# Half an output projection beside the last attention block, a router on un-normed rows, and GpSimd work in short pieces

## The chip, the cores and the metric

The kernel runs on one core of a Trainium2 chip. The metric is the device time of one execution in microseconds; the median of several executions counts. A core has TensorE (PE, matrix products into PSUM), VectorE (DVE), ScalarE (ACT), GpSimd (POOL) and SyncE (SP, which here only issues loads). Each engine works through its own instructions in order; semaphores make one engine wait for another.

## The reference

A decoder trunk of two layers on 1024 tokens (T) of width 1024 (D), all in float32. Cut to what matters here:

```python
for layer in range(DEPTH):
    if layer % 2 == 0:   # RWKV-7 (8 heads) and chunked GLA (4 heads)
        mix = concat([rwkv(h @ w_in), gla(h @ w_in)]) @ w_out
    else:                # S5 (32 groups) and chunked HGRN2 (4 heads)
        mix = concat([s5(h @ w_in), hgrn2(h @ w_in)]) @ w_out
    h = _layer_norm(DN_ALPHA * h + mix, ln1_g[layer], ln1_b[layer])
    ffn = _hierarchical_moe(h, ...)   # top-1 of 4 groups, top-2 of 8 experts in it
    h = _layer_norm(DN_ALPHA * h + ffn, ln2_g[layer], ln2_b[layer])

# GLA and HGRN2, per chunk: S <- diag(exp(b_last)) S + k_dec^T v;  o = (q exp(b)) S + scores v
# router: coarse = softmax(x @ wg + bg); fine = softmax(x @ we[group] + be[group])
```

## The kernel before, in words

The kernel is written with a tile framework. A planner in it gives every engine its order of instructions when the kernel is built, from the order of the program and a model of what each takes; so a line that is moved in the program may move work on all engines, and the order has to be read from the built program.

Float32 products are made from two parts. `split` (L104) rounds an operand to a "high" part on ScalarE (L106) and subtracts it to get the "low" part, on VectorE or, for weights of the input and output projections, on GpSimd (L107); three matmuls (hi·hi, lo·hi, hi·lo) then give one product. One weight part is 128 x 1024 elements; for the input projections it holds 8 slices of the contraction, for 128 output columns (`proj_T`, L164 to L166), 24 matmuls for 512 tokens.

A layer goes: mixers (tokens in two halves of 512, `n` = 0, 1), output projection with the first norm and the router (`out_ln1`, L685), routing (`route`, L781, whose second half, `overflow`, L878, places rows beyond an expert's capacity), 32 experts (`moe`, L1021), and `combine` with the second norm.

`gla_core` (L501) does a block of two heads (GLA) or one (HGRN2). For the levels s = 0, 1, 2, 4 ... 64 of a chunk of 128, TensorE makes the scores of the level (L522, L524) in PSUM banks of the ring "iv", VectorE copies them under a mask into the score tile (L532; the last level by ScalarE, L529), and VectorE multiplies gK and gQ for the next level by the decays (L541, L542). Then come the state (L551, L555) and the outputs (L560, L561), a norm of the output (L563 to L569), and a store to the scratch tensor `ydram` by GpSimd's queue (L76).

Before the last GLA block of layer 0, `last` frees the input projection's tiles, and `out_weights` (L674) loads the eight parts of the output weights (SP, L681; four raw buffers `oraw`) and splits them (ScalarE woh, GpSimd wol).

`out_ln1` then goes over eight tiles of 128 rows. `project` loads the residual row `or` (L692) and the mixers' outputs `oyr` from `ydram` (L694), splits them (oyh, oyl) and makes the product in two halves of 24 matmuls (L702 to L704); L705 adds the residual. `finish`, one tile behind, normalizes (`layer_norm`: statistics L661, L662, ScalarE L663, L664, L666, then VectorE's L667 and L668), stores the rows to `hdram`, transposes them (L716), and multiplies them with the router weights (L720, L721).

An expert's weights come as quarters of 128 x 1024, split by ScalarE and VectorE (`w_split`, `cut`) into two rings: the first HL quarters during `out_ln1`, the next HL2 when `moe` begins. `ex_in` transposes the gathered rows and makes xh and xl (L924 and after); `ex_up` (L938 to L940) multiplies. `keep` and `self.kept` chain instructions of an engine so that the planner leaves their order as written.

Of the kernel before, what the change touches and what calls it, by code (L numbers as in the profile page):

```python
# [20 lines left out]
D = 1024  # L21
NT = 8
# [13 lines left out]
class Kern:  # L36
# [67 lines left out]
    def split(self, hi, lo, src, lo_engine=None):  # L104
        nc = self.nc
        self.keep(nc.scalar.activation(hi, src, AF.Copy))  # L106
        self.keep((lo_engine or nc.vector).tensor_tensor(lo, src, hi.bitcast(F32), op=OP.subtract))  # L107
# [120 lines left out]
    def rwkv_setup(self):  # L228
# [14 lines left out]
        self.rwkv_consts(cst)  # L243
# [4 lines left out]
        lora = cst.tile([128, 2, 512], F32, name="lora")  # L248
# [9 lines left out]
        for i in range(2):  # L258
            Q, Zd = cst.tile([128, 8, 4, 64], F32, name=f"Q{i}"), cst.tile([128, 8, 2, 64], F32, name=f"Zd{i}")
# [241 lines left out]
    def gla_core(self, n, q, k, f, heads, S, norm_g, store):  # L501
# [8 lines left out]
        for s in (0, 1, 2, 4, 8, 16, 32, 64):  # L510
            L, R = (k if s < 2 else Ke), Q if s else q
            ps = [self.bank("iv", (128, 4, 128)) for _ in heads]
# [12 lines left out]
            for i, p in enumerate(ps):  # L525
                if s == 64:
                    nc.scalar.activation(SC[i][0:64, :, 64:], p[0:64], AF.Copy)
                elif s == 0:
                    nc.vector.tensor_tensor(SC[i], p, self.ident[:, None, :].to_broadcast([128, 4, 128]), op=OP.mult)  # L529
                else:  # L530
                    m = self.glev[s].rearrange("p (b t) -> p b t", t=s)[:, None].to_broadcast([128, 4, 64 // s, s])
                    nc.vector.copy_predicated(SC[i].rearrange("p c (b t) -> p c b t", t=2 * s)[:, :, :, s:], m,  # L532
                                              p.rearrange("p c (b t) -> p c b t", t=s))
            if s:
# [10 lines left out]
                nc.vector.tensor_tensor(d, d2[:, :, 0], d2[:, :, 1], op=OP.mult)  # L545
        kdT = self.token_major(Ke, "gkdT")
# [49 lines left out]
    def gla(self, n, hT, ydram, last):  # L596
# [17 lines left out]
        for blk in range(2):  # L614
# [40 lines left out]
    def layer_norm(self, pool, r, g, b, out, engine=None):  # L655
# [9 lines left out]
        nc.vector.scalar_tensor_tensor(rs[:, 1:2], mv[:, 0:1], -1.0, rs[:, 0:1], op0=OP.mult, op1=OP.mult)  # L665
        nc.scalar.activation(r, r, AF.Identity, scale=rs[:, 0:1], bias=rs[:, 1:2])  # L666
        nc.vector.tensor_tensor(r, r, g, op=OP.mult)  # L667
        (engine or nc.gpsimd).tensor_tensor(out, r, b, op=OP.add)  # L668
# [5 lines left out]
    def out_weights(self, l, w_out):  # L674

        es = ExitStack()
        pool = es.enter_context(self.tc.tile_pool(name=f"ow{l}", bufs=1, side="right", reuse_waits="tile"))
        raws = [pool.tile([128, D], F32, name=f"oraw{i}") for i in range(4)]
        W = [tuple(pool.tile([128, D], F32R, name=f"wo{x}{k}") for x in "hl") for k in range(KT)]
        for k in range(KT):  # L680
            self.nc.sync.dma_start(raws[k % 4], w_out[128 * k:128 * k + 128, :])  # L681
            self.split(W[k][0], W[k][1], raws[k % 4], self.nc.gpsimd)
        return es, W

    def out_ln1(self, l, src, ydram, W, hdram, ypool, pool):  # L685
# [3 lines left out]
        def project(i):  # L689
            ts = slice(128 * i, 128 * i + 128)  # L690
            r = pool.tile([128, D], F32, tag="or", bufs=3, name="or")
            nc.sync.dma_start(r, self.rows(src, i))  # L692
            yr = ypool.tile([128, KT, 128], F32, tag="oyr", bufs=2, name="oyr")
            nc.sync.dma_start(yr, ydram.rearrange("k p t -> p k t")[:, :, ts])  # L694
            yh = ypool.tile([128, KT, 128], F32R, tag="oyh", bufs=2, name="oyh")
            yl = ypool.tile([128, KT, 128], F32R, tag="oyl", bufs=2, name="oyl")
            self.split(yh, yl, yr)
            for q in range(2):
                ds_ = slice(512 * q, 512 * q + 512)
                p = self.bank("pj")  # L700
                for k, (wh, wl) in enumerate(W):
                    nc.tensor.matmul(p, yh[:, k, :], wh[:, ds_], start=(k == 0), stop=False)  # L702
                    nc.tensor.matmul(p, yh[:, k, :], wl[:, ds_], start=False, stop=False)  # L703
                    nc.tensor.matmul(p, yl[:, k, :], wh[:, ds_], start=False, stop=(k == KT - 1))  # L704
                nc.vector.scalar_tensor_tensor(r[:, ds_], r[:, ds_], ALPHA, p, op0=OP.mult, op1=OP.add)  # L705
            return r

        def finish(i, h):
            self.layer_norm(pool, h, g, b, h, nc.vector)
            self.store(self.rows(hdram, i), h)  # L710
# [10 lines left out]
            nc.vector.tensor_tensor(L[:, i, :], p[:, :36], bias, op=OP.add)  # L721

        for i in range(NT + 1):
            h = project(i) if i < NT else None
            if i == 0:
                g = self.bcast_row(pool, a["ln1_g"][l], "ln1g")
# [996 lines left out]
```

## Time and profile before

| what | value |
|---|---|
| median of 3 runs | 2972.58 us (2968.28 to 2976.91) |
| the profiled execution's own time | 2965.17 us |
| its span | 2963.4 us |
| TensorE busy | 2669.8 us (90% of the span) |
| VectorE busy | 2149.8 us (73%) |
| ScalarE busy | 1583.1 us (53%) |
| GpSimd busy | 739.3 us (25%) |
| granted TensorE clock, mean | 0.941 |

The stages of that execution: layer 0's mixers until about 770 us, its last GLA block 770 to 833, output projection and router 832 to 961, routing until 977, experts 987 to 1565, combine and layer 1's mixers until 2187, output stage 2147 to 2290, experts 2320 to 2893, combine until the end. In 40 equal slices of the span (tenths of busy time, 9 is 90% or more) the page shows:

```profile
PE   8999999999689699999997787879988799999995
DVE  5775447764444899999995658887554899999985
PEclk9999999999779799999998898889989899999998
```

A row of the timeline says when an instruction began and what it took; in brackets stands how long its engine had been idle and what ended that. A row with a count stands for several instructions in succession.

### The profile page before, as it was taken

What the parts mean: (1) busy time and instruction counts of PE and PEld (TensorE: products, weight loads), DVE (VectorE), ACT (ScalarE), POOL (GpSimd) and SP (SyncE); (2) the same over time, 40 slices, a digit from 0 to 9 for tenths busy, and PEclk for the clock granted to TensorE, in tenths of its full rate; (3) what the DMA queues carried; (4) which work ended last, traced back from release to release, by engine and by line L of the source; (5) the groups of instructions that cost most, each with busy time, mean ns of one, the idle gap of its engine ahead of it and who ended that gap; (6) DMA issues with size and microseconds to landing.
All of it is one profiled execution on the core that took longest, in us unless ns stands there. A gap on an engine that the chain in (4) does not pass through costs nothing.

```text
span 2963.4 us, 40755 instructions
## 1 busy us (share of the span) xinstructions
PE 2669.8 (90%) x15284; PEld 1977.1 (67%) x15284; DVE 2149.8 (73%) x3204; ACT 1583.1 (53%) x2292; POOL 739.3 (25%) x619
## 2 busy tenths in 40 slices
PE   8999999999689699999997787879988799999995
PEld 6766676666567477777774576667777577777772
DVE  5775447764444899999995658887554899999985
ACT  4342343333322588888883333334533588888873
POOL 4222222323300211111103454452130111111103
PEclk9999999999779799999998898889989899999998
DMA  3111131011253799999987322122343799999985
GB/s 109 30 37 33 43 87 38 27 29 47 78 175 140 256 376 379 375 380 376 382 334 223 96 74 57 44 69 74 127 153 135 275 376 378 382 383 378 381 315 196
DMA packets 234064, 581.52 MB, mean 196 GB/s; under 512 B 47534, under 2 KB 156167, under 8 KB 184711
## 3 DMA queue, kind: packets, MB, share of 16 engines
q1 hardware_dynamic: 211718, 518.03, 49.2%
q0 software_dynamic: 22144, 60.85, 5.8%
q8 instruction: 122, 2.00, 0.3%
q14 instruction: 80, 0.65, 0.1%
HBM read 541.97 MB, written 52.43 MB: 201 GB/s over the span
## 4 chain that ended last, share of the span: by engine, by line
issue 37%; PE 29%; DVE 12%; POOL 7%; ACT 2%; DMA 2%; POOLq 0%; SPq 0%; DVEq 0%; ACTq 0%
POOL xg L912 4%; PE bpj L164 3%; PE bpj L165 3%; PE bpj L166 3%; PE biv L522 2%; PE bpj L704 2%; PE bpj L702 2%; PE bpj L703 2%; POOL ybuf L976 2%; PE biv L414 1%; DVE gQ L542 1%; PE bpp L720 1%; PE bpo L171 1%; DVE gK L541 1%; DMA xg<-hdram,gi 1%
## 5 line engine op out<-in xcount | busy, mean ns | idle before, releaser
L107 DVE TENSOR_TENSOR mlo<-raw,mhi 128x1024 fp32r<-128x1024 f32 x768 | 923.9, 1222 | 109.2 <-ACT mhi L106 75.0
L106 ACT ACTIVATE mhi<-raw 128x1024 fp32r<-128x1024 f32 x768 | 805.9, 1059 | 201.6 <-PE bpo L969 87.2
L164 PE MATMUL bpj<-hT_hi,whi 128*128 128x512 f32 x736 | 310.7, 422 | 10.7 <-DVE hq L577 9.0
L107 POOL TENSOR_TENSOR wlo<-wraw,whi 128x1024 fp32r<-128x1024 f32 x92 | 221.5, 2409 | 392.7 <-ACT whi L106 324.5
L166 PE MATMUL bpj<-hT_hi,wlo 128*128 128x512 f32 x736 | 307.0, 417 | 9.4 <-POOL wlo L107 9.4
L165 PE MATMUL bpj<-hT_lo,whi 128*128 128x512 f32 x736 | 307.9, 418 | 0.0
L912 POOL DMA_INDIRECT xg<-hdram,gi x64 | 136.3, 2130 | 646.4 <-PE by L924 602.9
L106 ACT ACTIVATE whi<-wraw 128x1024 fp32r<-128x1024 f32 x92 | 97.1, 1057 | 233.2 <-PE bpj L165 161.7
L940 PE MATMUL bpj<-mhi,xl 128*96 128x512 f32 x512 | 203.5, 397 | 0.8 <-DVE xl L107 0.8
L938 PE MATMUL bpj<-mhi,xh 128*96 128x512 f32 x512 | 203.2, 397 | 0.0
L939 PE MATMUL bpj<-mlo,xh 128*96 128x512 f32 x512 | 202.7, 396 | 0.0
L938 PE MATMUL biv<-mhi,xh 128*96 128x512 f32 x512 | 201.8, 394 | 0.0
L939 PE MATMUL biv<-mlo,xh 128*96 128x512 f32 x512 | 201.6, 394 | 0.0
L940 PE MATMUL biv<-mhi,xl 128*96 128x512 f32 x512 | 201.6, 394 | 0.0
L164 PEld LDWEIGHTS bpj<-hT_hi,whi 128*128 128x128 f32 x736 | 143.9, 196 | 46.5 <-DVE hq L577 10.3
L166 PEld LDWEIGHTS bpj<-hT_hi,wlo 128*128 128x128 f32 x736 | 143.6, 195 | 40.9 <-POOL wlo L107 11.4
L165 PEld LDWEIGHTS bpj<-hT_lo,whi 128*128 128x128 f32 x736 | 143.5, 195 | 29.3 <-issue 3.5
L976 POOL DMA_INDIRECT ybuf<-yo,si x64 | 60.2, 940 | 385.2 <-ACT yo L975 375.5
L522 PE MATMUL biv<-gQ,gK 64*128 64x64 f32 (+1 forms) x640 | 76.1, 311 | 58.6 <-DVE gQ L542 58.6
L522 PEld LDWEIGHTS biv<-gQ,gK 64*128 64x128 f32 (+1 forms) x640 | 69.7, 222 | 74.3 <-issue 41.9
L704 PE MATMUL bpj<-woh,oyl 128*128 128x512 f32 x256 | 103.1, 403 | 7.8 <-DVE oyl L107 7.8
L940 PEld LDWEIGHTS bpj<-mhi,xl 128*96 128x96 f32 x512 | 83.4, 163 | 37.6 <-DVE xl L107 1.8
(608 smaller groups left out, 5717.0 us busy)
## 6 DMA issues: line engine op xcount, KB each, us to landing
raw<-in_moe_w_dram SPq DMA_DIRECT2D x384, 1024.0 KB
wraw<-in_ab_w_in_dram SPq DMA_DIRECT2D x50, 512.0 KB
wraw<-in_cd_w_in_dram SPq DMA_DIRECT2D x40, 512.0 KB
cy<-ybuf SPq DMA_DIRECT2D x16, 1024.0 KB
oyr<-ydram SPq DMA_DIRECT2D x16, 512.0 KB
hdram<-or POOLq DMA_DIRECT2D x16, 512.0 KB, 2.9
lnh<-hdram SPq DMA_DIRECT2D x16, 512.0 KB
ydram<-go POOLq DMA_DIRECT2D x16, 256.0 KB, 2.8
```

Of the source, the lines that this page charges most:

```text
L106: self.keep(nc.scalar.activation(hi, src, AF.Copy))
L107: self.keep((lo_engine or nc.vector).tensor_tensor(lo, src, hi.bitcast(F32), op=OP.subtract))
L164: nc.tensor.matmul(dst, wh[:, k, :], xh[:, k, :], start=(k == 0), stop=False)
L165: nc.tensor.matmul(dst, wh[:, k, :], xl[:, k, :], start=False, stop=False)
L166: nc.tensor.matmul(dst, wl[:, k, :], xh[:, k, :], start=False, stop=(k == KT - 1))
L522: nc.tensor.matmul(p[:, c, :], L[r, cc], rhs, start=True, stop=True)
L704: nc.tensor.matmul(p, yl[:, k, :], wh[:, ds_], start=False, stop=(k == KT - 1))
L912: self.nc.gpsimd.indirect_dma_start(out=xg[:CAP, :], out_offset=None, in_=hdram, in_offset=bass.IndirectOffsetOnAxis(ap=gidx, axis=0), bou ...
L938: self.keep(self.nc.tensor.matmul(p, xh[:, k, :], wh, start=(k == 0), stop=False))
L939: self.keep(self.nc.tensor.matmul(p, xh[:, k, :], wl, start=False, stop=False))
L940: self.keep(self.nc.tensor.matmul(p, xl[:, k, :], wh, start=False, stop=(k == KT - 1)))
L976: return nc.gpsimd.indirect_dma_start(out=ybuf, out_offset=bass.IndirectOffsetOnAxis(ap=sidx, axis=0), in_=y, in_offset=None, bounds_check ...
```

## The change

- **Short pieces.** GpSimd's low part of 128 x 1024 becomes four instructions of 128 x 256 (`lo_part`), and so does GpSimd's add of the second norm.
- **GLA levels.** The score banks get a ring "gs" with a turn of its own (the same two banks; four in the last GLA block of layer 0). The multiplies for the next level stand ahead of the masked copies of this one.
- **Output weights and early tiles.** The parts are loaded after the last block's core in program order (`out_early`), through two raw buffers. In layer 0 row tiles 0 to 3 (tokens 0 to 511) are projected there too. The other tiles run two ahead of `finish`, with four `or` buffers and one `oyr`.
- **Router.** `finish` transposes the un-normed row. The router weights are multiplied by ln1_g; sums of the weights and the part of ln1_b come from 16 matmuls with ones. The logits are p·rs + (sums·(-mu·rs) + bias), two VectorE operations. The norm is applied, and the row stored, after that.
- **First parts of the experts.** `cut` makes the high part and returns the low part as a function to be called. At the start of `moe` the low parts of the second ring come after `overflow`'s last multiply and after xl.
- RWKV constants, Q, Zd and lora move into a pool that is freed before the last block.

The diff, cut to its core:

```diff
+    def lo_part(self, hi, lo, src, lo_engine=None):
+        if lo_engine is None:
+            self.keep(self.nc.vector.tensor_tensor(lo, src, hi.bitcast(F32), op=OP.subtract))
+            return
+        hi, lo, src = (x if len(x.shape) == 2 else x.rearrange("p a b -> p (a b)") for x in (hi, lo, src))
+        n = hi.shape[1]
+        for i in range(0, n, n // 4):
+            s = slice(i, i + n // 4)
+            lo_engine.tensor_tensor(lo[:, s], src[:, s], hi[:, s].bitcast(F32), op=OP.subtract)
...
-            ps = [self.bank("iv", (128, 4, 128)) for _ in heads]
+            ps = [self.bank("gs", (128, 4, 128)) for _ in heads]
...
-    RINGS = dict(pj="ab", iv="cd", pp="e", po="f", y="g", ch="h")
+    RINGS = dict(pj="ab", iv="cd", gs="cd", pp="e", po="f", y="g", ch="h")
...
+        for i in range(0, D, D // 4):
+            s = slice(i, i + D // 4)
+            nc.gpsimd.tensor_tensor(out[:, s], r[:, s], b[:, s], op=OP.add)
...
-        raws = [pool.tile([128, D], F32, name=f"oraw{i}") for i in range(4)]
+        def part(k):
+            raw = p.tile([128, D], F32, tag="oraw", bufs=2, name="oraw")
+            self.nc.sync.dma_start(raw, w_out[128 * k:128 * k + 128, :])
+            self.split(W[k][0], W[k][1], raw, self.nc.gpsimd)
+        return es, W, part, pool
...
+    def out_early(self, l, src, ydram, weights, tiles):
+        es, W, part, pool = weights
         for k in range(KT):
+            part(k)
+        self.opool = pool("oe")
+        self.projected = {i: self.project(i, src, ydram, W, self.opool) for i in tiles}
...
         def finish(i, h):
-            self.layer_norm(pool, h, g, b, h, nc.vector)
-            self.store(self.rows(hdram, i), h)
+            rs = self.norm_stats(pool, h)
...
-            nc.vector.tensor_tensor(L[:, i, :], p[:, :36], bias, op=OP.add)
+            t = pool.tile([128, 36], F32, tag="lgt", bufs=2, name="lgt")
+            nc.vector.scalar_tensor_tensor(t, sums, rs[:, 1:2], bias, op0=OP.mult, op1=OP.add)
+            nc.vector.scalar_tensor_tensor(L[:, i, :], p[:, :36], rs[:, 0:1], t, op0=OP.mult, op1=OP.add)
+            self.norm_apply(h, rs, g, b, h, nc.vector)
+            self.store(self.rows(hdram, i), h)
+        done = self.projected
+        at = len(done)
+        for i in range(NT):
+            while at < min(NT, i + 2):
+                done[at] = self.project(at, src, ydram, W, self.opool)
+                at += 1
+            finish(i, done.pop(i))
...
-        for j in range(HL, HL + HL2):
-            cut(j)
+        low = [cut(j) for j in range(HL, HL + HL2)]
...
+        self.kept = {self.last_over.ins.engine: self.last_over}
         more()
-        self.kept = {}
+        for f in low:
+            f()
...
             def last():
                 es.close()
                 close()
+                self.rings["gs"] = "cdeh"
...
+            ahead()
...
+                        lambda: self.out_early(0, x, yd[0], weights[0], range(4)))
...
+        self.out_early(1, mid, yd[1], weights[1], ())
```

TensorE in the last GLA block of layer 0. bgs and biv are the score banks, by the state and output banks, woh and wol the output weights' parts, oyh and oyl those of a row tile. Before, the block's matmuls stand by themselves:

```order
L522 MATMUL biv<-gQ,gK 128x64 x40
L524 MATMUL biv<-gQ,gK 64x64 x8
L496 MATMUL biv<-ident,gK 128x128 x4
L551 MATMUL by<-gV,gkdT 64x128 x8
L560 MATMUL by<-gQ,glS 128x128
```

Now:

```order
L533 MATMUL bgs<-gQ,gK 128x64 x24
L728 MATMUL bpj<-woh_7071,oyh 128x512
L729 MATMUL bpj<-wol_7072,oyh 128x512
L728 MATMUL bpj<-woh_7071,oyh 128x512
L729 MATMUL bpj<-wol_7072,oyh 128x512
L533 MATMUL bgs<-gQ,gK 128x64 x8
L730 MATMUL bpj<-woh_7071,oyl 128x512
L728 MATMUL bpj<-woh_7073,oyh 128x512
L729 MATMUL bpj<-wol_7074,oyh 128x512
L533 MATMUL bgs<-gQ,gK 128x64 x8
```

The first weight parts of tile 0 now stand between the levels, ahead of the levels 16, 32 and 64; farther on the block's state stands behind the fifth part, its outputs behind the sixth and seventh, and the matmul of its last norm behind the eighth. Tiles 1 to 3 follow it.

VectorE at the end of `out_ln1`, from the last tile's aggregate to the first operation of routing. Before:

```order
L662 BN_AGGR lnmv<-lnst 128x2
L721 TENSOR_TENSOR logits<-bpp,gbias 128x36
L665 SCALAR_TENSOR_TENSOR lnrs<-lnmv,lnrs 128x1
L667 TENSOR_TENSOR or<-or,ln1g 128x1024
L668 TENSOR_TENSOR or<-or,ln1b 128x1024
L721 TENSOR_TENSOR logits<-bpp,gbias 128x36
L794 TENSOR_REDUCE mx<-logits 128x8
```

Now:

```order
L678 SCALAR_TENSOR_TENSOR lnrs<-lnmv,lnrs 128x1
L686 TENSOR_TENSOR or<-or,ln1b 128x1024
L787 SCALAR_TENSOR_TENSOR lgt<-gsums,lnrs,gbias 128x36
L684 TENSOR_TENSOR or<-or,ln1g 128x1024
L788 SCALAR_TENSOR_TENSOR logits<-bpp,lnrs,lgt 128x36
L686 TENSOR_TENSOR or<-or,ln1b 128x1024
L852 TENSOR_REDUCE mx<-logits 128x8
```

The last logits stand between the two passes of the norm, no longer behind both and the transposes.

VectorE at the start of the experts (om and rm are `overflow`'s last steps, mlo the low part of an expert's weights, xl that of the gathered rows). Before:

```order
L107 TENSOR_TENSOR mlo<-raw_8136,mhi 128x1024
L895 CAST exi<-ex 128x22
L901 SCALAR_TENSOR_TENSOR blk<-blk,rq 128x16
L107 TENSOR_TENSOR mlo<-raw_8136,mhi 128x1024
L904 TENSOR_TENSOR om<-e_1080,blk 128x336
L107 TENSOR_TENSOR mlo<-raw_8138,mhi 128x1024
L905 TENSOR_TENSOR rm<-om,v_8029 128x336
L107 TENSOR_TENSOR xl<-bch,xh 128x384
```

Now:

```order
L959 SCALAR_TENSOR_TENSOR blk<-blk,rq 128x16
L953 CAST exi<-ex 128x22
L962 TENSOR_TENSOR om<-e_1095,blk 128x336
L963 TENSOR_TENSOR rm<-om,v_8255 128x336
L111 TENSOR_TENSOR xl<-bch,xh 128x384
L111 TENSOR_TENSOR xl<-by,xh 128x384
L919 SCALAR_TENSOR_TENSOR emiv<-biv,slotp 96x21
L111 TENSOR_TENSOR mlo<-raw,mhi 128x1024
```

All eight low parts of the second ring stand behind xl.

## Rows read from the trace of the kernel before

**Rows 1.** Windows: busy us of PE, PEld, DVE, ACT, POOL; granted clock; DMA share; GB/s.

```profile
770.00:833.00 63.00, 36.50 (x201) 26.94 (x199) 25.27 (x37) 17.19 (x23) 23.02 (x14) 0.56 0.33 103
...
841.00:948.00 107.00, 106.63 (x526) 88.86 (x527) 52.32 (x77) 27.17 (x42) 3.74 (x7) 0.98 0.41 137
...
1000.00:1550.00 550.00, 548.83 (x2570) 396.62 (x2569) 499.39 (x490) 457.61 (x550) 86.74 (x58) 1.00 0.99 373
...
1720.00:2000.00 280.00, 224.03 (x1272) 184.36 (x1271) 225.00 (x416) 95.30 (x169) 139.15 (x99) 0.90 0.21 58
```

**Rows 2.** Timeline, end of the last GLA block of layer 0: start, duration, engine, line, operation.

```profile
832.94 0.54 POOL L76 DMA_DIRECT2D ydram<-go  x1 [6.18 <-DVE go L611]
...
841.19 0.80 PE L704 MATMUL bpj<-woh,oyl 128*128 128x512 f32 x1 [7.83 <-DVE oyl L107]
```

**Rows 3.** Timeline, the same block's first part: the output weights and two VectorE multiplies.

```profile
777.08 16.94 POOL L107 TENSOR_TENSOR wol<-oraw,woh 128x1024 fp32r<-128x1024 f32 x7 [11.70 <-ACT woh L106]
...
779.47 7.62 SPq L681 DMA_DIRECT2D oraw<-in_ab_w_out_dram  x4
...
783.18 1.06 ACT L106 ACTIVATE woh<-oraw 128x1024 fp32r<-128x1024 f32 x1 [3.35 <-DMA oraw<-in_ab_w_out_dram]
...
784.45 2.57 DVE L542 TENSOR_TENSOR gQ<-gQ,gD 128x256 f32<-128x256 f32 x1
...
797.43 0.42 DVE L542 TENSOR_TENSOR gQ<-gQ,gD 128x256 f32<-128x256 f32 x1
```

**Rows 4.** Timeline, two neighbouring matmuls of the projection at full clock.

```profile
947.75 0.39 PE L703 MATMUL bpj<-wol,oyh 128*128 128x512 f32 x1
...
947.97 0.40 PE L704 MATMUL bpj<-woh,oyl 128*128 128x512 f32 x1
```

**Rows 5.** Timeline, end of the output stage of layer 0: last tile, router, first routing operation.

```profile
948.41 0.69 DVE L705 SCALAR_TENSOR_TENSOR or<-or,bpj 128x512 f32<-128x512 f32 x1 [4.03 <-PE bpj L704]
...
954.35 1.23 DVE L668 TENSOR_TENSOR or<-or,ln1b 128x1024 f32<-128x1024 f32 x1
...
955.62 1.12 PE L716 MATMUL bpp<-ident,or 128*128 128x128 f32 x4 [4.15 <-DVE or L668]
...
961.32 0.19 DVE L794 TENSOR_REDUCE mx<-logits 128x8 f32<-128x32 f32 x1
```

**Rows 6.** Timeline, start of the expert stage of layer 0.

```profile
985.32 0.88 PE L924 MATMUL bch<-ident,xg 96*128 96x96 f32 x4 [9.37 <-DMA xg<-hdram,gi]
...
986.30 0.49 ACT L106 ACTIVATE xh<-bch 128x384 fp32r<-128x384 f32 x1 [17.05 <-PE bch L924]
...
990.16 0.55 DVE L107 TENSOR_TENSOR xl<-bch,xh 128x384 fp32r<-128x384 f32 x1
...
991.53 0.72 PE L940 MATMUL bpj<-mhi,xl 128*96 128x512 f32 x1
```

**Rows 7.** Groups of instructions, whole span, shapes kept apart: count, busy us, mean ns, idle before.

```profile
L107 POOL TENSOR_TENSOR wlo<-wraw,whi 128x1024 fp32r<-128x1024 f32 x92 | 221.5, 2409 | 392.7 <-ACT whi L106 324.5 <-PE bpj L166 29.8 <-PE biv L522 19.6
...
L540 POOL COPY gK<-hk 128x256 f32<-128x256 f32 x8 | 6.7, 837 | 18.0 <-DVE hk L1249 18.0
...
L541 DVE TENSOR_TENSOR gK<-gK,gD 128x256 f32<-128x256 f32 x72 | 51.2, 711 | 6.0 <-PE biv L524 6.0
```

**Rows 8.** Timeline, HGRN2 beside S5 in layer 1: GpSimd operations back to back, and VectorE.

```profile
1804.47 1.17 POOL L1464 TENSOR_TENSOR stmp<-s5C,s5PI 128x576 f32<-128x576 f32 x1
...
1804.87 1.05 DVE L541 TENSOR_TENSOR gK<-gK,gD 128x256 f32<-128x256 f32 x1
...
1805.72 1.47 POOL L1465 TENSOR_TENSOR sCA<-sCA,stmp 128x576 f32<-128x576 f32 x1
```

**Rows 9.** What TensorE waited for in layer 1's mixers, 1720 to 2145 us.

```profile
PE biv L522 <- DVE gQ L542: 23.6, 16, 8.3
...
PE bpj L166 <- POOL wlo L107: 6.6, 2, 4.5
```

**Rows 10.** The same for layer 0's mixers, 40 to 770 us.

```profile
PE biv L522 <- DVE gQ L542: 10.2, 7, 4.4
```

**Rows 11.** Timeline, last HGRN2 block of layer 1.

```profile
2153.04 1.94 PE L522 MATMUL biv<-gQ,gK 128*128 128x64 f32 x8 [4.80 <-DVE gQ L542]
```

More of the change, by code (lines that the diff above doesn't have):

```diff
@@ new lines, in part, with project @@
+        def part(k):
[3 more added lines that the diff above has]
+        return es, W, part, pool
+    def project(self, i, src, ydram, W, pool):
+        nc = self.nc
+        ts = slice(128 * i, 128 * i + 128)
+        r = pool.tile([128, D], F32, tag="or", bufs=4, name="or")
+        nc.sync.dma_start(r, self.rows(src, i))
+        yr = pool.tile([128, KT, 128], F32, tag="oyr", bufs=1, name="oyr")
+        nc.sync.dma_start(yr, ydram.rearrange("k p t -> p k t")[:, :, ts])
+        yh = pool.tile([128, KT, 128], F32R, tag="oyh", bufs=2, name="oyh")
+        yl = pool.tile([128, KT, 128], F32R, tag="oyl", bufs=2, name="oyl")
+        self.split(yh, yl, yr)
+        for q in range(2):
+            ds_ = slice(512 * q, 512 * q + 512)
+            p = self.bank("pj")
+            for k, (wh, wl) in enumerate(W):
+                nc.tensor.matmul(p, yh[:, k, :], wh[:, ds_], start=(k == 0), stop=False)
+                nc.tensor.matmul(p, yh[:, k, :], wl[:, ds_], start=False, stop=False)
+                nc.tensor.matmul(p, yl[:, k, :], wh[:, ds_], start=False, stop=(k == KT - 1))
+            nc.vector.scalar_tensor_tensor(r[:, ds_], r[:, ds_], ALPHA, p, op0=OP.mult, op1=OP.add)
+        return r
@@ L686, in out_ln1 @@
+    def out_ln1(self, l, src, ydram, W, hdram, pool):
         nc, a = self.nc, self.a
         L = self.rpool.tile([128, NT, 36], F32, name="logits")
[L689 to L706, printed above, removed]
@@ new lines, in out_ln1 @@
+        for x, j in ((wb, 1), (wge, 0)):
+            nc.vector.tensor_tensor(x, wge, gb[:, j, :, None].to_broadcast([128, KT, 36]), op=OP.mult)
+        bias = pool.tile([128, 36], F32, name="gbias")
+        nc.sync.dma_start(bias[:, 0:4], a["moe_bg"][l].rearrange("(o n) -> o n", o=1).to_broadcast([128, 4]))
+        nc.sync.dma_start(bias[:, 4:], a["moe_be"][l].rearrange("g e -> (g e)").rearrange("(o n) -> o n", o=1).to_broadcast([128, 32]))
+        p = self.bank("pp")
+        for j, x in enumerate((wge, wb)):
+            for k in range(KT):
+                nc.tensor.matmul(p[:, 36 * j:36 * j + 36], self.ones, x[:, k, :], start=(k == 0), stop=(k == KT - 1))
@@ L708, in finish @@
+        sums = pool.tile([128, 36], F32, name="gsums")
+        nc.vector.tensor_copy(sums, p[:, 0:36])
+        nc.vector.tensor_tensor(bias, bias, p[:, 36:72], op=OP.add)
         def finish(i, h):
-            self.layer_norm(pool, h, g, b, h, nc.vector)
-            self.store(self.rows(hdram, i), h)
+            rs = self.norm_stats(pool, h)
             hT = pool.tile([128, KT, 128], F32, tag="ohT", bufs=2, name="ohT")
@@ L1018, in cut @@
         if j < 2 * len(self.halves):
-            self.parts[j] = self.w_split(self.raws[j // 2], j % 2, self.halves[j // 2][0].shape[1])
+            self.parts[j], low = self.w_split(self.raws[j // 2], j % 2, self.halves[j // 2][0].shape[1])
+            return low
+        return lambda: None
     def moe(self, l, pool, gi, si, exi, hdram, ybuf):
@@ L1102, in moe_more @@
                 for z in range(4):
-                    self.ex_up(x, ph[w], z, self.w_split(raws[w][z // 2], z % 2, 512))
+                    part, low = self.w_split(raws[w][z // 2], z % 2, 512)
+                    low()
+                    self.ex_up(x, ph[w], z, part)
             raws.append([self.w_load(ws[2], q) for q in range(2)])
@@ L1110, in moe_more @@
             for z in range(4):
-                self.ex_down(h, py, z, self.w_split(raws[2][z // 2], z % 2, 1024))
+                part, low = self.w_split(raws[2][z // 2], z % 2, 1024)
+                low()
+                self.ex_down(h, py, z, part)
             self.ex_out(py, ix[:, 1:2], ybuf)
```

102 lines of the change are left out of this document (51 added, 51 removed).

## The prediction

> **What bounds the kernel now.** I read the 40 slices of the page first: TensorE is busy 90% of the span, so a change can only win where its row drops below 9. Then the stages one by one. In the expert stage TensorE is busy 548.8 of 550 us at full clock with the DMA engines at 0.99 [rows 1]: nothing of the change can shorten that stage itself, only the way into it. The output projection of layer 0 is also a full stretch: 106.6 of 107 us from 841 to 948. What lies idle is the stretch before it, the last GLA block of layer 0 (770 to 833), where TensorE works 36.5 of 63 us at a granted clock of 0.56, and layer 1's mixers, where it works 224 of 280 us and VectorE 225 [rows 1].
>
> The timeline says why the projection starts only at 841: the block's last result is stored at 832.94, and the next real matmul waits for VectorE's oyl, which had waited for the load of that store [rows 2]. Row tiles 0 to 3 need nothing of this block: it computes tokens 512 to 1023. Then the waits in the mixers: the longest sum in layer 1 is for gQ, a VectorE multiply, 23.6 us in 16 waits, the largest 8.3 [rows 9]; in layer 0 the same line stands with 10.2 us [rows 10].
>
> **Projection of four tiles beside the last block (layer 0).** A tile is 8 weight parts x 3 matmuls x 2 halves = 48 matmuls, 0.22 to 0.23 us apart at full clock [rows 4], so 10.8 us; four are 43 us. The question is when these four are done. The added price is that the weights now pass through 2 raw buffers, not 4, and that by the new order TensorE meets them between the block's levels. One buffer's round [rows 3]: high part 1.06 us, low part 16.94/7 = 2.42, and 3.7 us from the re-load's issue (779.47) to the next high part (783.18), together 7.2 us. Two buffers give a part each 3.6 us. The first low part ends at 779.5; the eighth then at 779.5 + 7 x 3.6 = 804.7, where before the queue was through at about 796.5 (a part per 2.42 us). By the order the block's last norm matmul stands behind the eighth part of tile 0, so its store goes out near 812 instead of 832.94, and with the 8 us from store to matmul [rows 2], tiles 4 to 7 can start from about 820. Tile 0 ends near 807. Tiles 1 to 3 follow without a wait, 32.4 us and some 2 us for a clock still low at their start: 842. So at 842 four tiles are left, where before at 841.2 all eight were left: 43 - 1 = **42 us gained**. Does the block itself fit? Its 36.5 us of TensorE work were at 0.56 of the clock, about 20 us at full clock [rows 1]; with 10.8 of tile 0 that is 31 us for the 34 us from 771 to 805 if the clock rises, so this is tight. Bounds: -50 (everything dense at full clock from 771: 20 + 43 us of work end at 834) and -22 (clock and weights hold tile 0 until about 826).
>
> **Router from un-normed rows.** Before, the last tile's transposes wait 4.15 us for the normed row, and routing begins at 961.32 [rows 5]. Now they need only the residual sum, which is ready 0.69 us after 948.41. The transposes, copies and small matmuls then run beside the norm's chain, and what stays ahead of routing on VectorE is that chain, whose last add ends at 954.35 + 1.23 = 955.6 [rows 5]. So routing starts 5.7 us earlier; the two small operations on 36 columns take the place of one. The row's store is not in the way: routing lasts until the gather. Per layer -5.5, **together -11** (-6 to -12; layer 1 by the same code). The 16 added matmuls with ones and the scaled router weights stand among other work; I cost them at nothing. If that cover were gone, they would cost 16 matmuls of 36 columns, under 4 us per layer by the pitch of [rows 4].
>
> **First parts of the experts.** The gathered rows arrive at 985.32, but VectorE makes xl only at 990.16, behind overflow operations and weight low parts mixed with them; the first matmul on xl is at 991.53 [rows 6]. In the new order xl comes ahead of the low parts of the second ring. It could start after the transposes (0.88 us) and one copy (0.49 us), 986.7; add the same 1.37 us from xl to matmul: 988.1. **-3 per layer, -6** (0 to -8). The low parts pushed back are VectorE's; it has 50.6 us to spare in the 550 us behind [rows 1], and if that were not enough, TensorE would wait at the second expert for what was gained here.
>
> **Short pieces.** VectorE's multiply takes 0.42 us alone and 2.57 us while GpSimd works through the weights' low parts [rows 3]; the mean of 72 is 0.71 [rows 7]. A GpSimd low part holds 2.41 us, 92 times, for the input weights alone [rows 7]. Does a waiting VectorE get in between two GpSimd operations that stand back to back? The trace says yes [rows 8]: the multiply at 1804.87 ends 1805.92, just behind the GpSimd operation that ended at 1805.64, though the next one was queued. A piece of 128x256 is bounded by 0.60 us (a quarter of 2.41) and by 0.84 us (a copy of this size, which shares the time with VectorE) [rows 7]; I take 0.65, by the first, since it is the same operation. So the longest single wait falls from 2.1 us to about 0.6. It doesn't vanish: a chain of VectorE operations meets four short waits instead of one. I take half of what TensorE waits for gQ: **-12 in layer 1** of 23.6 [rows 9], **-5 in layer 0** of 10.2 [rows 10]. In layer 1's last block, where two waits in a row are like the one of 4.80 us [rows 11], **-5**. The multiplies that now stand ahead of the copies of the same level, and the score banks of their own, are in these numbers. Bounds of the three together: 0 and -42 (all of [rows 9, 10] and 8 us of the last block).
>
> The Trainium skill, page "SBUF — State Buffer", section "Who interferes with whom", says that a VectorE instruction with two SBUF inputs and a GpSimd instruction that reads SBUF exclude each other, and that the one that issues first has the port pair for its whole instruction. By that rule the time held by four pieces is the time held by one long instruction, so a VectorE that always has such an operation waiting would lose as much as before; the sum would then be without these 22 us. The 2.57 and 0.42 us agree with the exclusion; how much VectorE has in between that can run beside GpSimd, no single row shows.
>
> LN2's add in pieces lies behind VectorE, which is the busier there; at the very end it may cost or give 1 us. GpSimd's added overhead costs nothing while it idles ahead of 92 parts for 393 us [rows 7].
>
> **Sum.** -42 - 11 - 6 - 22 = -81 us against the profiled execution's 2965.17 us (span 2963.4), 2884. That execution is 7.4 us below the median of the runs shown, 2972.58; against this median the forecast is **2891 us**.
>
> **The rivals.**
> - *Weights and in-order queues take the wait's place in the last block.* TensorE, ScalarE and GpSimd run in order; with two buffers and the weights between the levels, a level's copies stand behind a high part that waits for a load. For it: the re-load took 3.7 us [rows 3], and the clock was 0.56 [rows 1]. Against: the first four tiles' 32 us behind tile 0 hide a late block. Then -22 instead of -42: 2911.
> - *Pieces only divide the same blocking.* VectorE is at 225 of 280 us in layer 1 [rows 1], so it nearly always has something waiting. Against it: [rows 8], and the 2 x 2.57 us pattern of back-to-back parts. Without the 22 us: 2913; with the first rival too, 2933.
> - *Slower: the low parts come too late.* Place: GpSimd's queue in both layers' mixers. Each weight part feeds 24 matmuls, 5.4 us at full clock [rows 4]. If each piece must first wait for VectorE, and four pieces take more than 5.4 us, that is over 1.35 us each, TensorE waits for wlo at every part. At 1.57 us each, 92 x (6.28 - 5.4) = 81 us eat the whole gain; at 1.7 us it is 129 us and 3020 us. For it: two waits for wlo already, 6.6 us [rows 9]. Against: 0.60 to 0.84 us per piece [rows 7].
> - *The change does nothing:* the early tiles only push the block's end back by their own time, and the rest is lost in noise. Against: 26.5 idle us in the block and 8 behind it [rows 1, 2].
>
> **How the numbers follow.** Forecast 0.58, weights 0.17, pieces 0.18, no change 0.03, slower 0.04. About 0.3%, 9 us, is what a measurement of this kernel can tell from no change. The low end takes the gains' bounds, -50 - 12 - 8 - 42 = -112: 2861, and 5 us for the spread of the runs: 2856. The high end takes in both first rivals at once (2933) and 2 us: 2935. Faster 0.93, within 0.3% 0.03, slower 0.04.
>
> **What would show it.** Right: the first matmul of tile 4 near 842, eight low parts done by 806, TensorE's clock above 0.56 from 771 on; routing begins within 7 us after the last projection matmul; the first xl matmul within 3 us of the gathered rows' transposes; the mean of the gK multiply near 0.55 instead of 0.71 us, pieces of 0.6 to 0.8 us, and less than 15 us of waits for gQ in layer 1. Wrong: TensorE waiting for wol or woh between the levels for over 10 us, the gK mean unchanged, waits for wlo of many times 1 us, or an expert stage that no longer runs at full busy time.

## The result, and the profile after

The changed kernel took 2888.06 us (median of 4 runs, 2884.93 to 2889.38) against 2971.56 us before: ratio 0.9716, 95% interval 0.9699 to 0.9733. The forecast was 2891 us in 2856 to 2935. The sum was right to 3 us; its terms were not, as the stages show. Each column of the table is one execution; the stages are cut at events that both traces have: the first score matmul of the last GLA or HGRN2 block, the last matmul of the output projection, the first operation of routing, the first and last matmul on xl.

| stage (us, profiled executions) | before | after | difference | forecast |
|---|---|---|---|---|
| start to layer 0's last block | 773.3 | 748.6 | -24.7 | -5 |
| last block to last projection matmul | 174.7 | 142.4 | -32.3 | -42 |
| to routing | 13.4 | 9.1 | -4.3 | -5.5 |
| routing to first xl matmul | 30.2 | 23.8 | -6.4 | -3 |
| experts, first to last xl matmul | 565.2 | 569.3 | +4.1 | 0 |
| to layer 1's last block | 587.2 | 572.7 | -14.5 | -12 |
| last block to last projection matmul | 133.0 | 137.1 | +4.1 | -5 |
| to routing | 13.3 | 10.2 | -3.1 | -5.5 |
| routing to first xl matmul | 30.2 | 23.5 | -6.7 | -3 |
| experts | 564.6 | 570.0 | +5.4 | 0 |
| to the end of the span | 78.3 | 78.9 | +0.6 | 0 |
| sum | 2963.4 | 2885.5 | -77.9 | -81 |

**The mixers.** Groups of the changed kernel's whole span, shapes apart (count, busy us, mean ns, idle before):

```profile
L118 POOL TENSOR_TENSOR wlo<-wraw,whi 128x256 fp32r<-128x256 f32 x368 | 282.4, 797 | 323.0 <-ACT whi L106 309.3 <-PE bpp L182 4.3 <-DMA wraw<-in_ab_w_in_dram 4.2
...
L543 DVE TENSOR_TENSOR gK<-gK,gD 128x256 f32<-128x256 f32 x72 | 35.8, 497 | 35.0 <-PE bgs L533 26.0 <-PE bgs L535 6.9 <-POOL wlo L118 1.2
```

A part now holds GpSimd for 4 x 0.80 = 3.19 us where it was 2.41, and yet the multiply's mean fell from 0.71 to 0.50 us [rows 7]; the pieces are not alone in this, as the experiments show. What TensorE waited for in layer 0's mixers, first of the kernel before (further lines of the view of [rows 10]), then of the changed one:

```profile
PE biv L496 <- DVE gK L541: 4.0, 2, 2.1
PE bch L436 <- DVE SV L450: 3.9, 3, 1.8
PE biv L414 <- DVE T L422: 3.5, 3, 1.5
```
```profile
PE bgs L533 <- DVE gQ L544: 2.1, 6, 0.6
...
PE bch L447 <- DVE SV L461: 0.4, 1, 0.4
PE biv L425 <- DVE T L433: 0.3, 1, 0.3
```

Not only the waits for gQ went (10.2 to 2.1 us): those for gK, and for SV and T in the RWKV chain, 11.4 us together, went almost wholly. From its first matmul at 5.4 us to the last block TensorE stands still for 44.4 us before and for 19.7 now, while its busy time is the same (723.5 and 723.6 us): the 24.7 us are waits.

**Layer 0's last block and the projection.** Timeline of the changed kernel:

```profile
762.77 1.06 ACT L106 ACTIVATE woh<-oraw 128x1024 fp32r<-128x1024 f32 x1 [1.83 <-DMA oraw<-in_ab_w_out_dram]
773.74 0.65 ACT L550 ACTIVATE gSC<-bgs 64x256 f32<-64x256 f32 x2 [9.91 <-PE bgs L535]
774.28 1.05 ACT L106 ACTIVATE woh<-oraw 128x1024 fp32r<-128x1024 f32 x1
...
775.41 6.56 POOL L118 TENSOR_TENSOR wol<-oraw,woh 128x256 fp32r<-128x256 f32 x8 [7.15 <-ACT woh L106]
...
787.19 2.78 POOL L118 TENSOR_TENSOR wol<-oraw,woh 128x256 fp32r<-128x256 f32 x4 [0.40 <-ACT woh L106]
...
826.53 1.87 PE L769 MATMUL bpp<-wge,ones 128*128 128x36 f32 x16
```

The fourth high part is made at 762.77, the fifth only at 774.28: ScalarE, in order, stands at the score copies of the last level, for which it waits 9.91 us. The eighth low part ends at 789.97, 41.3 us after the block's start. Tile 3 ends at 826.5, 77.9 us after it. In windows of the same stretch the clock is this (columns as in [rows 1]):

```profile
759.00:769.00 10.00, 8.63 (x51) 6.79 (x51) 6.98 (x11) 2.11 (x2) 7.72 (x9) 0.50 0.64 220
769.00:779.00 10.00, 9.41 (x60) 6.74 (x58) 3.54 (x11) 4.08 (x6) 3.59 (x6) 0.71 0.50 159
779.00:789.00 10.00, 9.34 (x41) 6.35 (x41) 1.69 (x2) 3.98 (x5) 7.86 (x11) 1.00 0.52 158
```

From 759 to 769 TensorE was busy 86% of the time, at the lower of its two clock levels, 1.2 GHz; about 775 the upper level, 2.4 GHz, came back.

**The end of the output stage**, changed kernel, timeline around the last tile:

```profile
891.08 0.40 PE L730 MATMUL bpj<-woh,oyl 128*128 128x512 f32 x1
...
892.93 1.24 ACT L683 ACTIVATE or<-or,lnrs 128x1024 f32<-128x1024 f32 x1
...
894.06 0.29 ACT L676 ACTIVATE lnrs<-lnmv,eps 128x1 f32<-128x1 f32 x1
...
895.62 0.19 ACT L677 ACTIVATE lnrs<-lnrs 128x1 f32<-128x1 f32 x1
...
899.01 1.22 DVE L686 TENSOR_TENSOR or<-or,ln1b 128x1024 f32<-128x1024 f32 x1
900.14 0.18 DVE L852 TENSOR_REDUCE mx<-logits 128x8 f32<-128x32 f32 x1
```

As in the forecast, the norm's last add (899.01) is what routing waits for. But ScalarE takes the seventh tile's norm (892.93) ahead of the eighth's logarithm (894.06), and the copies of the transposes ahead of its exponential (895.62): the chain from the last matmul is 9.1 us, where before the norm's chain ended 7.6 us after that matmul, a part of the 13.4 us [rows 4, 5].

**The start of the experts**, changed kernel:

```profile
920.41 0.88 PE L982 MATMUL bch<-ident,xg 96*128 96x96 f32 x4 [6.01 <-DMA xg<-hdram,gi]
...
921.90 0.56 DVE L111 TENSOR_TENSOR xl<-bch,xh 128x384 fp32r<-128x384 f32 x1 [1.43 <-ACT xh L106]
...
923.94 0.63 PE L998 MATMUL bpj<-mhi,xl 128*96 128x512 f32 x1
...
941.42 0.72 PE L1017 MATMUL biv<-ident,hid 96*128 96x96 f32 x4 [3.77 <-DVE hid L1009]
```

xl follows the rows in 1.5 us, where it took 4.8 [rows 6]. Then TensorE stands 3.77 us for the first expert's hidden rows, which VectorE makes late, and behind this wait the granted clock is 0.51 from 942.0 to 945.5.

### The profile page after: what moved, and what is told of

The parts are those of the page before. It is cut to its first block, busy times and chain, and to the rows that moved or that the text cites. A ratio compares the mean times of both kernels' runs of the same rounds, so it can differ in the third digit from the quotient of the medians.

```text
span 2885.5 us, 41351 instructions
## 1 busy us (share of the span) xinstructions
PE 2670.9 (93%) x15348; PEld 1980.4 (69%) x15348; DVE 2100.3 (73%) x3228; ACT 1586.0 (55%) x2292; POOL 819.5 (28%) x991
## 4 chain that ended last, share of the span: by engine, by line
issue 36%; PE 32%; DVE 10%; POOL 8%; DMA 2%; ACT 2%; POOLq 0%; SPq 0%; DVEq 0%; ACTq 0%
POOL xg L970 4%; PE bpj L176 4%; PE bpj L177 4%; PE bpj L175 4%; PE bgs L533 3%; POOL ybuf L1034 2%; PE bpj L729 2%; PE bpj L730 2%; PE bpj L728 2%; PE biv L425 1%; PE bpp L785 1%; PE bpo L182 1%; PE biv L1220 1%; PE by L571 1%; PE by L572 1%
## 5 line engine op out<-in xcount | busy, mean ns | idle before, releaser
L118 POOL TENSOR_TENSOR wlo<-wraw,whi 128x256 fp32r<-128x256 f32 x368 | 282.4, 797 | 323.0 <-ACT whi L106 309.3
L729 PE MATMUL bpj<-wol,oyh 128*128 128x512 f32 x256 | 105.8, 413 | 4.2 <-POOL wol L118 4.2
L997 PEld LDWEIGHTS bpj<-mlo,xh 128*96 128x96 f32 x512 | 84.2, 164 | 36.5 <-issue 0.2
L996 PEld LDWEIGHTS bpj<-mhi,xh 128*96 128x96 f32 x512 | 84.1, 164 | 35.9 <-issue 0.2
```

The costliest lines, as they stand in the source:

```text
L118: lo_engine.tensor_tensor(lo[:, s], src[:, s], hi[:, s].bitcast(F32), op=OP.subtract)
L996: self.keep(self.nc.tensor.matmul(p, xh[:, k, :], wh, start=(k == 0), stop=False))
L997: self.keep(self.nc.tensor.matmul(p, xh[:, k, :], wl, start=False, stop=False))
```

## The experiments

All ratios are against the kernel before, run on the same chip; the changed kernel's is 0.9716 (0.9699 to 0.9733). The kernel before took 2968.6 to 2977.3 us (medians) on the chips of these runs, so runs are compared by ratio. "The change" is the kernel after. The router's edit, the late low parts of the experts and the ring "gs" were not undone by themselves.

### Whole pieces, pieces alone, two pieces, eight pieces

```diff
-        for i in range(0, n, n // 4):
-            s = slice(i, i + n // 4)
+        for i in range(0, n, n):        # e1_whole; n // 2: e10_two; n // 8: e11_eight
+            s = slice(i, i + n)
```

The second run is the kernel before with `lo_part`'s loop of four pieces in `split`, and nothing else.

Whole: 

> The change with one edit undone: GpSimd's low part is again one instruction of 128x1024 (LN2's add stays in pieces). Theory A: the 24.6 us by which the last GLA block of layer 0 begins earlier, and the 14.5 us of layer 1's mixers, come from the short pieces; then that block begins near 770 again, the mean of the gK multiply is back near 0.7 us, and the time is 30 to 40 us longer, 2918 to 2928. Rival B: they come from the multiplies that stand ahead of the masked copies, and from the score banks of their own; then the time stays within 8 us of 2888.

Pieces alone: 

> The kernel before with the short low parts of GpSimd alone. Theory A: the mixers of both layers gain nearly all of what the whole change gained there, 24.6 and 14.5 us, and layer 1's last block some 3 us more: 2930 to 2938. Rival B: under 10 us, 2962 to 2972. If pieces and level order need each other, this run gains little and the undoing of the pieces costs much.

Two: 

> The change with GpSimd's low part in two pieces of 128x512 instead of four of 128x256. If what VectorE loses goes with the length of one GpSimd instruction (2.41 us whole, 0.80 us as a quarter, some 1.3 us as a half), the 47 us between whole and quarters divide as 1.1 to 0.5: 13 to 18 us longer than with four, 2901 to 2906. Rival: it is enough that one VectorE operation gets in between, and two pieces do nearly as well, 2886 to 2893.

Eight: 

> The change with eight pieces of 128x128. By the length of one instruction a further gain of 5 to 10 us, 2878 to 2883. Rival: each instruction has a fixed share, since a quarter took 0.80 us and not 0.60; eight pieces then hold GpSimd for 4 us or more per part, the low parts come later, and the time is the same or up to 10 us longer, 2886 to 2898.

Measured: whole 2934.79 us, ratio 0.9862 (0.9816 to 0.9909); pieces alone 2908.84 us, 0.9782 (0.9735 to 0.9829); two 2904.90 us, 0.9767 (0.9743 to 0.9791); eight 2898.51 us, 0.9731 (0.9709 to 0.9754). By the ratios pieces alone take 2.2% off the kernel before, all the other edits without them 1.4%, and both 2.8%: some 0.7%, about 20 us, can be had by either, but with two of the ratios known to 0.5% only, its size is loose. Theory A holds in both runs, and both forecasts were too small: the pieces are worth 1.5% to 2.2%. Its signs for the run with whole pieces came only in part: the gK mean went back to 0.60 us, not 0.7, and with pieces alone it is 0.59; the other edits shorten this multiply too. The stages of the router and of the way to xl are as before with pieces alone (13.4 and 30.2 us in layer 0) and as in the change with whole pieces (8.8 and 23.9 us): these gains are not the pieces'.

In the pieces' run layer 0's last block begins at 740.1 us, 33 earlier than before, and layer 1's mixers take 567.9 us, 19 less. The traces tell apart how long TensorE stands still in the mixers and how long it is busy, which moves with its granted clock (us; one execution each, layer 0 from 5.4 us on):

| run | layer 0: still | busy | granted clock | layer 1: still |
|---|---|---|---|---|
| before | 44.4 | 723.5 | 0.967 | 103.4 |
| pieces alone | 22.3 | 712.5 | 0.986 | 92.7 |
| change, whole pieces | 33.2 | 743.2 | 0.950 | 101.9 |
| change, two pieces | 25.5 | 730.4 | 0.966 | 96.6 |
| change, four pieces | 19.7 | 723.6 | 0.975 | 91.8 |
| change, eight pieces | 16.4 | 729.0 | 0.966 | 88.0 |

TensorE stands still for less time the shorter the pieces are, in both layers. The waits for gQ in layer 0 (10.2 us) fall to 3.4 with pieces alone and to 3.8 with the other edits alone, so here either can give the same gain; those for SV and T (3.9 and 3.5) stay at 3.5 each as long as the pieces are whole. The block of the run with whole pieces begins at 781.8 instead of the 770 that was expected because TensorE's busy time is longer there, at a lower clock; that execution is also the slowest of its four. How much of the clock is the pieces' doing stays open: in seven executions whose code is that of the change up to this block, its start lies between 742.1 and 748.6 us with 19.2 to 20.0 us of standing still.

What GpSimd's pieces take, whole span, of the runs with two and with eight:

```profile
L118 POOL TENSOR_TENSOR wlo<-wraw,whi 128x512 fp32r<-128x512 f32 x184 | 244.2, 1346 | 338.2 <-ACT whi L106 328.9 <-PE bpp L182 4.3 <-PE bpj L177 3.0
```
```profile
L118 POOL TENSOR_TENSOR wlo<-wraw,whi 128x128 fp32r<-128x128 f32 x736 | 350.3, 511 | 288.4 <-ACT whi L106 278.8 <-PE bpp L182 4.3 <-PE bpj L177 3.0
```

With 2413 ns (x92) of the run with whole pieces and the 797 of quarters this is close to a line, 250 ns and 2.1 ns per column. From whole to quarters the ratio falls by 1.5%; two pieces give 0.5% of it back, as the length of one instruction would have it. Eight are no better than four (0.9731 against 0.9716, intervals that overlap): the rival holds, at the edge of its range. A part holds GpSimd for 4.1 us, and though TensorE waits less in the mixers, layer 0's eighth output-weight part ends 46.9 us after the block's start instead of 41.3, and that stage is 148.0 us long instead of 142.4.

### The old order of a level

```diff
+            for i, p in enumerate(ps):      # masked copies first, as before
...
             if s:                           # then the multiplies
...
-            for i, p in enumerate(ps):
...
```

> The change with the old order of a level: masked copies first, then the multiplies (the ring of score banks stays new). Theory A: little, 0 to 8 us more, 2888 to 2896, and most of it in the last blocks. Rival B: 25 to 35 us more, 2913 to 2923, with the waits for gQ back near 10 us in layer 0 and 20 us in layer 1.

Measured 2881.25 us (2875.63 to 2895.26), 0.9677 (0.9629 to 0.9725). That is below both ranges, and its interval holds the change's ratio: the order of a level gives nothing that these runs can tell, and rival B is out. Waits for gQ are a little longer with the old order in layer 0 (3.4 us, 2.1 with the new):

```profile
PE bgs L533 <- DVE gQ L553: 3.4, 5, 0.9
```

### Without early tiles, in two ways

```diff
-                        lambda: self.out_early(0, x, yd[0], weights[0], range(4)))
+                        lambda: self.out_early(0, x, yd[0], weights[0], ()))
...
+        o = [4, 5, 6, 7, 0, 1, 2, 3] if l == 0 else list(range(NT))   # e9_late_tiles only
```

First edit alone: 

> The change without the four early row tiles of layer 0; the weights are still loaded beside the last block, and all eight tiles are projected in the output stage. If the early tiles fill time that would be idle, as the prediction put it, the output stage of layer 0 gets longer by about 36 to 43 us: 2924 to 2931. If the early tiles only displaced the block's own work (its outputs are stored 49 us after its start, against 60 before), the loss is under 25 us, below 2913.

Both: 

> The change with the row tiles of layer 0 in the order 4 to 7, 0 to 3 and none projected early, so that no projection matmul can stand before the last block's end (in the run without early tiles the planner had still put tile 0 between the levels and tiles 1 and 2 right behind). If the early tiles are worth the 42 us of the prediction: 2926 to 2932. Rival: without them the block itself ends sooner, its result stored near 45 us after its start instead of 49, eight dense tiles from about 53 us on need 107 us, and the stage is 160 us long instead of 142: a loss of 14 to 22 us, 2902 to 2910.

Measured: the first 2895.81 us, 0.9731 (0.9684 to 0.9778); with late tiles 2916.23 us, 0.9796 (0.9776 to 0.9817). The first edit did not do what I meant: `out_ln1` projects two tiles ahead, and the planner put tile 0 between the levels all the same. With late tiles the stage is 170.3 us, 28 more than 142.4 (142.4 to 143.8 in four executions that share this stage): this is what the early tiles are worth, neither 42 nor the rival's 14 to 22. The reckoning closes: four tiles are 43 us, and with them the first four were done 77.9 us after the block's start, 14.7 later than the 63.2 at which the late ones begin. The rival fails on its premise too. Timeline of that run, whose block began at 747.4:

```profile
795.66 0.54 POOL L76 DMA_DIRECT2D ydram<-go  x1 [4.74 <-DVE go L622]
...
803.77 3.63 PE L769 MATMUL bpp<-wge,ones 128*128 128x36 f32 x16 [11.31 <-DVE wge L762]
806.36 1.06 ACT L106 ACTIVATE oyh<-oyr 128x1024 fp32r<-128x1024 f32 x1 [12.50 <-DMA oyr<-ydram]
...
810.62 0.77 PE L728 MATMUL bpj<-woh,oyh 128*128 128x512 f32 x1
```

The result is stored 48.3 us after the block's start, as with the early tiles among its levels (48.8), so they don't slow the block. The projection starts 15 us behind the store: first comes the load of `oyr`, then the router's matmuls with ones (803.77, L769), which now have nothing to hide behind.

### Raw buffers of the output weights

```diff
-            raw = p.tile([128, D], F32, tag="oraw", bufs=2, name="oraw")
+            raw = p.tile([128, D], F32, tag="oraw", bufs=4 if l else 2, name="oraw")   # e5, the change
...
-        raws = [pool.tile([128, D], F32, name=f"oraw{i}") for i in range(4)]
+        raws = [pool.tile([128, D], F32, name=f"oraw{i}") for i in range(2)]           # e8, before; k % 2
```

Four in layer 1: 

> The change with four raw buffers for the output weights of layer 1 (two stay in layer 0). Theory: layer 1's output stage gained nothing (147.3 us from the last block's start to routing, 146.4 before) because two buffers bring the eighth part 41 us after the block's start, not 33; then this run has it at 33 to 35 again and gains 5 to 9 us: 2879 to 2883. Rival: the granted clock, low while TensorE waits for the block's multiplies, sets the length; then less than 3 us.

Two in the kernel before: 

> The kernel before with two raw buffers for the output weights instead of four, nothing else. Theory of the buffers: in layer 1 the eighth part comes near 41 us after the last block's start instead of 33.3, and the time is 4 to 8 us longer, 2976 to 2980; in layer 0 the later parts are hidden, since the projection waits for the last block's result until 841 anyway. Rival: no difference beyond 2 us in either layer.

Measured: 2882.83 us, 0.9710 (0.9691 to 0.9728), and 2961.84 us, 0.9971 (0.9958 to 0.9984). In layer 1 both follow the theory by the trace: with four the eighth part comes at 33.9 us and the stage is 130.1 us long instead of 137.1; with two in the kernel before it comes at 39.7 and the stage is 2.6 us longer. By the total times alone the 5 us are inside the intervals. In layer 0 the kernel before went against my expectation: with two buffers the stage is 164.9 us, 9.8 shorter than with four. The block's result is stored 53.6 us after its start instead of 59.7, which is 6.1 of the 9.8 us. GpSimd now pauses between parts, and VectorE's multiplies pass in the pauses:

```profile
785.28 2.35 POOL L107 TENSOR_TENSOR wol<-oraw,woh 128x1024 fp32r<-128x1024 f32 x1 [2.40 <-ACT woh L106]
...
786.29 1.62 DVE L541 TENSOR_TENSOR gK<-gK,gD 128x256 f32<-128x256 f32 x1
...
787.84 0.41 DVE L542 TENSOR_TENSOR gQ<-gQ,gD 128x256 f32<-128x256 f32 x1
```

With four buffers the parts stood back to back, and two multiplies in a row took 1.58 us and 2.57 us [rows 3]; the first of them, in the kernel before:

```profile
782.95 1.58 DVE L541 TENSOR_TENSOR gK<-gK,gD 128x256 f32<-128x256 f32 x1
```

That the pauses are the whole cause is read from the traces and was not tested by itself.

### The low parts at the start of the experts

```diff
-        for f in low:
+        for f in low[:5]:
...
+                    if not e:
+                        after.extend(low[5:])   # behind the first expert's hidden rows
```

> The change with the last three of the eight low parts of the experts' second ring after the first expert's hidden rows on VectorE. Theory: the start of the experts is 6 us shorter in each layer, but 4 to 5 us come back because VectorE, late by eight low parts, makes the first hidden rows late (TensorE waits 3.8 us for them). Then the wait is gone or under 1 us and each layer gains 2 to 4 us: 2880 to 2884. Rival: the lateness only moves to the second expert's low parts, and the time is the same within 2 us.

Measured 2887.12 us, 0.9718 (0.9705 to 0.9732): nothing. The rival holds. What TensorE waited for at the start:

```profile
PE bpj L997 <- DVE mlo L111: 2.7, 1, 2.7
PE biv L1017 <- DVE hid L1009: 1.3, 1, 1.3
```

The 3.8 us have become 2.7 for a low part and 1.3 for the hidden rows. VectorE is full there (in the change, busy 18.4 of the 20 us from 920 on): before, it made five of the low parts while the rows were still on their way.

### Together, and the copies of the last level

`e7_both` has the edits of e5 and e6; the last run has that of e5 and

```diff
-                if s == 64:
+                if s == 64 and self.rings["gs"] == "cdeh":
+                    nc.vector.tensor_copy(SC[i][0:64, :, 64:], p[0:64])
+                elif s == 64:
```

Both: 

> Both edits together: four raw buffers in layer 1 and the three late low parts. If the two theories hold and do not overlap, the gains add up: 2871 to 2879. If either fails, its share is missing.

Copies: 

> Four raw buffers in layer 1 as before, and in the last GLA block of layer 0 the score copies of level 64 on VectorE instead of ScalarE. Theory: the eighth output weight part came 41.3 us after the block's start and not 31 because ScalarE, in order, held the fifth high part behind these copies for some 10 us though its load had landed; then the fifth part no longer waits for the level, the eighth comes at 33 to 37 us, the output stage of layer 0 is 138 to 140 us long instead of 142 to 144, and with layer 1's 5 to 7 us the time is 2876 to 2880. Rival: TensorE's own order, tile 0 between the levels at the low clock, sets the length; the parts come earlier but the stage stays at 142 to 144 us and the time at 2881 to 2883, that of four buffers in layer 1 alone.

Measured: 2881.35 us, 0.9689 (0.9675 to 0.9704): e5's share alone, as e6 had failed. With the copies on VectorE 2878.56 us (2874.61 to 2880.1), 0.9690 (0.9676 to 0.9703), the lowest median; by the ratio it is 0.26% below the change, with intervals that still overlap a little, and level with e7's, so the copies' own share does not show in the total time. ScalarE in that run:

```profile
765.91 1.06 ACT L106 ACTIVATE woh<-oraw 128x1024 fp32r<-128x1024 f32 x1 [4.54 <-DMA oraw<-in_ab_w_out_dram]
772.11 0.60 ACT L509 ACTIVATE gkdT<-biv 128x512 f32<-128x512 f32 x1 [5.15 <-PE biv L507]
772.61 1.05 ACT L106 ACTIVATE woh<-oraw 128x1024 fp32r<-128x1024 f32 x1
```

The block began at 746.6: the fifth part comes at 19.3 us instead of 25.6, but the sixth now stands behind the next copy of the block (772.11, gkdT), the eighth low part still ends at 39.2 us, and the stage is 140.3 us. So taking these copies off ScalarE brings only 2 to 3.5 us (the stage is 142.4 to 143.8 us in four executions with them), because the next copies take their place. The ends of the low parts tell more. In the changed kernel the fourth ends 2.6 us later after the block's start than forecast (19.6 against 6.2 + 3 x 3.6 = 17.0), the fifth 9.0 us later (29.6), the eighth 9.9: 6.4 us come where ScalarE stands at the copies. In the last run the fifth ends at 23.6, the sixth at 30.9, again behind a copy on ScalarE. The re-load of the fifth part took 4.3 us there from its issue, not longer; by that the fifth part's data lay ready near 768.5 in the changed kernel (an estimate from 764.20 + 4.3), so the copies held it some 6 us, not the 10 that was expected.

## Why the prediction was right

The total was right because errors of both signs met. Point by point, by its own steps:

- **What bounds the kernel:** right. The expert stage stayed at its length but for its start. The gains lie in the stretches that were named, but layer 0's mixers, the second largest, were named with 5 us.
- **Early tiles, -42:** mechanism right, size wrong: 28 us by the run with late tiles. The step that failed is "the eighth at 779.5 + 7 x 3.6 = 804.7", 31 us after the block's start; it came at 41, since I let the parts follow their buffers alone and not ScalarE's queue. The first rival named that queue the other way round, copies behind a high part; here a high part stood behind copies, and 6.4 us of the delay arose there. These 10 us are what the stage lacks (-32.3); that the tiles are worth only 28 is because without them the stage would already be 4 us shorter than before. "Tight" for the clock was right: it stayed low until about 775. The 16 matmuls with ones, costed at nothing, stand bare between tile 3 and tile 4, from 826.5 to about 830, as 32 instructions; the bound of 4 us was their price.
- **Router, -11:** -7.4. The chain was named rightly; the previous tile's norm and the transposes' copies ahead of it on ScalarE were left out.
- **First parts, -6:** the way to xl became 6.4 and 6.7 us shorter, twice the forecast (3.3 us of it because the gather took 4.4 us from issue to transposes, not 7.7; why, no run tested), and 4.1 and 5.4 us came back in the experts. The text put this wait at the second expert and trusted 50.6 us spare in 550; but in the first 20 us VectorE has 1.6 to spare. Nothing in the sum stood for this.
- **Short pieces, -22:** far too low for layer 0's mixers (24.7 against 5), near for layer 1's (14.5 against 12, in part by luck: the waits for gQ, which it was worked out from, fell by 8.2, from 23.6 to 15.4), wrong for layer 1's last block. There the pieces alone did bring 6.0 us (127.0 against 133.0), near the 5 of the forecast, but two raw buffers cost 7 us, and the text had charged them in layer 0 only. The failing step for the mixers is "half of what TensorE waits for gQ": it priced one line of the view, and of that a half, where SV, T and gK wait behind the same GpSimd parts.
- **The rivals:** the weights' in-order queues did take 10 us, half of that rival's 20. "Pieces only divide the same blocking" fell with the run of pieces alone. Low parts that come too late: no, a quarter took 0.80 us, far from 1.35. The Trainium skill's rule ("SBUF — State Buffer", section "Who interferes with whom") that the first to issue has the port pair for its instruction agrees with these traces, 0.42 against 2.57 us. What I worked out from it, that a VectorE that always has such an operation waiting would lose as much, does not: no gK or gQ multiply of layer 0's last block took over 0.96 us, and pieces alone took 2.2% off the time.
- **The signs:** pieces of 0.80 us and the gK mean came as said, though that mean fell by other edits too. The eighth part (41 us after the block's start, forecast 33), routing (9.1 us after the last matmul, forecast 7), the first matmul on xl (3.5 us behind the transposes' start, forecast 3) and the waits for gQ in layer 1 (15.4 us, forecast under 15) missed.

## What to carry to other kernels

Where one engine's operation waits for another engine's instruction to end, as VectorE's multiplies did here, the length of that instruction is the price, and cutting it can gain even though the background work gets a third longer; two, four and eight pieces should be tried, since each has a fixed share. Price a stall by every wait behind the same blocker, and a stream of weights by every in-order queue that it passes, not by its buffers alone. Before a difference between two traces is put down to an edit, part it into standing still and busy time, since the second moves with the clock. Where a planner sets the order, taking an edit away may leave its effect in place: read the order again before such an experiment is believed.

## What the runs showed of the hardware

GpSimd's subtraction took 2413, 1346, 797 and 511 ns for 1024, 512, 256 and 128 columns: about 250 ns for each instruction beside 2.1 ns per column, while VectorE was working. TensorE stood at the lower level of its clock, 0.50, in a stretch in which it was busy 8.63 of 10 us with score matmuls of 64 columns, projection matmuls of 512 and short waits between them. Fewer buffers for a transfer made the kernel before faster by 0.3% (0.9958 to 0.9984); its trace has pauses between GpSimd's instructions where there were none.
